# When weights are split while a layer norm's first half is turned: a hold with two levels

## The chip, the cores and the metric

The kernel runs on one core of a Trainium2 chip. The metric is the device time of one execution in microseconds (us). Before the change it is 2224.89 us, the median of 3 runs (2224.24 to 2225.13).

A core has engines that work through their own queues in order and wait for each other by semaphores: TensorE (PE, matrix products; PEld is its weight load), VectorE (DVE), ScalarE (ACT), GpSimd (POOL) and SyncE (SP), which here only issues DMAs.

## The reference, cut to what matters

One layer of an encoder over 256 rows of 2048 columns, in float32:

```python
x = layer_norm(ALPHA * x + 0.5 * swiglu(x, ffn1_w1, ffn1_w3, ffn1_w2), ln1_g, ln1_b)
mix = hybrid_mixer(x, w_in, b_gates, conv_w, norm_g, w_up_m, w_up_sb, w_out)
x = layer_norm(ALPHA * x + mix, ln2_g, ln2_b)
x = layer_norm(ALPHA * x + 0.5 * swiglu(x, ffn2_w1, ffn2_w3, ffn2_w2), ln3_g, ln3_b)
x = x + sigmoid(x @ w_ple_gate) * (p @ w_ple_proj)
```

`layer_norm` needs the mean and the variance of a whole row of 2048, so nothing that follows a norm can start for a row before the last column of that row is there. `swiglu` has an inner width of 5632.

## The kernel before, in words

**Products.** The 256 rows are two halves of 128 (t = 0, the first half, and t = 1, the second). A weight matrix is cut into tiles of 256 by up to 512 (512 KB), called weights below; each is used by one unit for each half. A float32 product is made of three products of a shorter format: every operand is split into a hi part (its rounded value) and a lo part (the rest), and a unit is two times three matmuls: hi by hi (L1115), hi by lo of the weight (L1116), lo of the activation by hi (L1117). Weights are split by `split_one`: ACT casts the raw tile to hi (L1064), DVE subtracts to get lo (L1068). Activations lie transposed in `actT` tiles, one for 512 columns (a chunk, c = 0 to 3) of one half; two weights use one chunk.

**Order.** The program is recorded by a Python scheduler that writes the units for PE in a fixed list and, between two units, whatever else is due by its planned clock (`Sched`, `DELAY`). Since every engine works in the order of recording, this decides what stands ahead of what on DVE and ACT. After each unit `splits_due` records splits as long as the number of split weights that still have a use (`splits`) is below a limit from `limits`: 5 in a feed-forward stage, 6 in the mixer, 11 within 8 weights of a border between stages, and 8 while `held[0]` is set. A unit whose weight isn't split yet forces it (`split_one` in the main loop). `loads` records the DMAs of raw weights up to another limit; it is called from `split_one`.

**A norm.** There are three: norm 1 between the first feed-forward part and the mixer, norm 2 between the mixer and the second feed-forward part, norm 3 between that and the last stage. Ahead of a norm, the last 8 units of the first half come before the last 8 of the second half for norms 1 and 3; after it, the first 8 weights are used for the first half, then for the second. For each half: DVE adds the finished product onto `xres` (L548, or L926 at norm 2) and takes statistics of 512 columns (L413); after the fourth, `finish` records BN_AGGR (L419), a square root on ACT (L238, out `rstd`), the reciprocal (L422) and the four scalings (L426). Then `turn` records for each chunk four transposes on PE (L436, into a PSUM bank `ms`), four ACTIVATEs on ACT (L238, scale and shift), the cast to hi on ACT (L442), and, 2.6 us later by the planned clock, the lo part on DVE (L444). `finish` sets `held[0]`, and the eighth lo part (`self.left == 0`) clears it. So splits of the next stage's weights are recorded between the steps of the norm, up to 8.

**The last stage** starts with four small products for each half (`w_ple_proj`, one weight each), whose results ACT copies from PSUM (L971); only then come the products of the normed rows with `w_ple_gate`.

Of the kernel before, what the change touches and what calls it, by code (L numbers as in the profile page):

```python
# [31 lines left out]
RAW_FFN, RAW_MIX, RAW_EDGE, RAW_HELD = 16, 5, 4, 8  # L32
SPLIT_FFN, SPLIT_MIX, SPLIT_EDGE, SPLIT_HELD = 5, 6, 11, 8
# [147 lines left out]
def kernel(  # L181
# [25 lines left out]
    def temp():  # L207
        sched.until(lambda: temps[0] < TEMP_BUFS)
        temps[0] += 1
        return temp_pool.tile([P, COL], F32, name="temp", tag="temp")  # L210

    def drop(n=1):
        temps[0] -= n

    def misc(shape):
        return ps_pool.tile(shape, F32, name="ms", tag="ps")
# [1 line left out]
    def big(shape=(P, 1024)):  # L218
        return page_pool.tile(list(shape), F32, name="big", tag="page")

    pages, held = [0], [False]

    def act_tile():
        pages[0] += 1
# [11 lines left out]
    def activate(out, in_, func, **kw):  # L236
        use_table(func)
        nc.scalar.activation(out, in_, func, **kw)  # L238
# [35 lines left out]
    def whole(act, c, t):  # L274
        if c not in act.whole:
            act.whole[c] = big()
            pages[0] += 1
        return act.whole[c][:, t * COL:(t + 1) * COL]

    def finished(act, c, t):  # L280
        act.mark(c, t, 4)
        if act.forms and all(act.ready(c, h) for h in range(TT)):
            sched.spawn(form_turn(act, c), DELAY["form"] + 3.0 * c)
# [97 lines left out]
    class Norm:  # L381
# [35 lines left out]
        def finish(self, t):  # L417
            mv = small.tile([P, 2], F32, name="mv", tag="mv")
            nc.vector.bn_aggr(out=mv[:], in_=self.stats[t][:])  # L419
            rstd = small.tile([P, 1], F32, name="rstd", tag="rstd")  # L420
            activate(rstd[:], mv[:, 1:2], ACT.Sqrt, bias=eps[:, 0:1])
            nc.vector.reciprocal(out=rstd[:], in_=rstd[:])  # L422
            held[0] = True
            for c in range(4):
                xs = xres[t][:, c * COL:(c + 1) * COL]
                nc.vector.tensor_scalar(out=xs, in0=xs, scalar1=mv[:, 0:1], scalar2=rstd[:, 0:1],  # L426
                                        op0=ALU.subtract, op1=ALU.mult)
                sched.spawn(self.turn(t, c), DELAY["ln_turn"] + DELAY["ln_step"] * c)
            return
            yield  # L430

        def turn(self, t, c):
            act = self.act
            ps = misc([P, 4, P])
            for k in range(4):
                nc.tensor.transpose(ps[:, k], xres[t][:, (4 * c + k) * P:(4 * c + k + 1) * P], ident[:])  # L436
            y = whole(act, c, t) if act.forms else temp()[:]
            for k in range(4):
                g, b = (self.gb[:, i, 4 * c + k:4 * c + k + 1] for i in range(2))
                activate(y[:, k * P:(k + 1) * P], ps[:, k], ACT.Identity, scale=g, bias=b)  # L440
            dst, y = act.get(c, t), y.rearrange("q (k s) -> q k s", s=P)
            nc.scalar.copy(dst[:, 0], y)  # L442
            yield DELAY["ln_low"]
            nc.vector.tensor_tensor(out=dst[:, 1], in0=y, in1=dst[:, 0], op=ALU.subtract)  # L444
            if not act.forms:
                drop()
            finished(act, c, t)
            self.left -= 1
            if self.left == 0:
                held[0] = False  # L450
                sched.spawn(self.rows(), self.delay)

        def rows(self):
# [21 lines left out]
    def ffn(w1, w3, w2, act, norm, skew=True, ahead=()):  # L475
# [9 lines left out]
        def up(c):  # L485
            s = {}

            def gate(ps, t):
                s[t] = temp()
                activate(s[t][:], ps, ACT.Silu)  # L490

            def hidden(ps, t):
                nc.vector.tensor_tensor(out=s[t][:], in0=ps, in1=s[t][:], op=ALU.mult)
                sched.spaced(turn(s[t], c, t), DELAY["h"] + 2.0 * t, TURN_GAP)

            return group(w1, range(0, D, 2 * P), c * COL, COL, act, gate), group(w3, range(0, D, 2 * P), c * COL, COL, act, hidden)

        def up7(c):
# [5 lines left out]
            def done(m, banks):  # L504
                ps = {k: v["ps"][:] for k, v in banks.items() if v}
                if m == 5:
                    e = temp()
                    nc.scalar.copy(e[:], ps["E"])
                    banks["B"]["ps"], banks["W"]["ps"] = seeded
                    both(banks["B"]["ps"][:], ps["X"], e[:], ALU.subtract)  # L510
                    drop()
                elif m == 6:
                    nc.scalar.copy(banks["W"]["ps"][:], ps["B"])
                elif m == 4:
                    s[1] = temp()
                    nc.scalar.copy(s[1][:], ps["E"])
                elif m == 2:
                    s[0] = temp()
                    sched.spawn(silu(s[0], ps["X"]), DELAY["silu"])
                elif m == 7:  # L520
                    both(s[1][:], ps["W"], s[1][:], ALU.add)
                    sched.spawn(silu(s[1], s[1][:]), DELAY["silu"])
                elif m == 3:
                    nc.vector.scalar_tensor_tensor(out=s[0][:], in0=ps["B"], scalar=-1.0, in1=s[0][:],
                                                   op0=ALU.mult, op1=ALU.mult)
                    sched.spaced(turn(s[0], c, 0), DELAY["h"], TURN_GAP)
                    sched.spawn(late(ps["W"]), DELAY["late"])
# [6 lines left out]
            def late(w):  # L534
                nc.vector.scalar_tensor_tensor(out=s[1][:], in0=w, scalar=-1.0, in1=s[1][:],
                                               op0=ALU.mult, op1=ALU.mult)
                sched.spaced(turn(s[1], c, 1), DELAY["h"], TURN_GAP)
                return
                yield
# [74 lines left out]
    def sb_columns(ps, t, first, count):  # L614

        for which in range(3):
            lo, hi = max(first, 8 * which), min(first + count, 8 * which + 8)
            if lo >= hi:
                continue
            name = ("sq", "sk", "sv")[which]  # L620
            src = ps[:, (lo - first) * DS:(hi - first) * DS]
            if which == 2:
                if (name, t) not in st:
                    st[name, t] = big()
                cs = slice((lo - 16) * DS, (hi - 16) * DS)
                nc.scalar.copy(st[name, t][:, cs], src)
                flags.update((name, t, h - 16) for h in range(lo, hi))
            else:
                stage = temp()
                nc.scalar.copy(stage[:, :(hi - lo) * DS], src)  # L630
                sched.spawn(sb_turn(name, t, stage, lo - 8 * which, hi - lo), DELAY["sbt"])
# [238 lines left out]
    for n in (4, 4, 4, 4, 4, 2):  # L870
        program.extend(flat(group(w_in, range(0, D, 2 * P), sq0 + first * DS, n * DS, x1T,
                                  lambda ps, t, f=first, n=n: sb_columns(ps, t, f, n))))
# [145 lines left out]
    def limits(j):  # L1018

        if held[0]:  # L1020
            return RAW_HELD, SPLIT_HELD
        if any(-EDGE <= j - e < EDGE for e, _ in edges):
            return RAW_EDGE, SPLIT_EDGE
        mixer = [m for e, m in edges if e <= j][-1:] == [True]
        return (RAW_MIX, SPLIT_MIX) if mixer else (RAW_FFN, SPLIT_FFN)
# [4 lines left out]
    def loads(most=len(raws)):  # L1030
        while (pos["load"] < most and pos["raw"] < (4 if pos["at"] < 6 else limits(pos["split"])[0])
               and (mixing() or pages[0] + pos["raw"] + 2 * max(limits(pos["split"])[1], len(splits)) < PAGES - SPARE)):
            j = pos["load"]
            r = raws[j]
            r.tile = page_pool.tile([P, 2, COL], F32, name="raw", tag="page")
            for ks in pieces(j):
                nc.sync.dma_start(out=r.tile[:, ks, :r.cols], in_=r.src[:, ks])
                if j == 0 and ks.start == 0:
                    load_x(0, 1)
            if r.plus is not None:  # L1040
                nc.gpsimd.dma_start(out=r.tile[:, :, :r.cols], in_=r.plus, accum_op=ALU.add)
            pos["load"] += 1
            pos["raw"] += 1
# [33 lines left out]
    def splits_due():  # L1077
        most = pos["at"] + 3 if pos["at"] < 8 else len(weights)
        while pos["split"] < most and len(splits) < limits(pos["split"])[1]:
            split_one()  # L1080
# [74 lines left out]
```

## Time and profile before

| | before |
|---|---|
| median of 3 runs | 2224.89 us |
| the profiled execution, its own time | 2225.94 us |
| its span, first to last instruction | 2224.2 us |
| PE busy | 2201.7 us (99%) |
| DVE busy | 1684.0 us (76%) |
| ACT busy | 1268.5 us (57%) |
| POOL busy | 187.2 us (8%) |
| chain that ended last: PE's share | 95% |
| mean granted TensorE clock | 0.996 |

The profiled execution is 1.05 us above the median, and 1.74 us of its time lie outside the span. PE is busy nearly throughout, so a change can take time away only where PE stands still or runs at a lower granted clock. Views by time show which lines stand there; a row of such a view has the start in us from the start of the span, the length, the engine, the line, the operation with its tiles and how many were merged, and in brackets the idle time before it and what ended it.

### The profile page before, as it was taken

Reading aid. Unit: us, or ns where it says so; the run is one execution under the profiler, and the core shown is the slowest. Engines: PE = TensorE matmul, PEld = TensorE weight load, DVE = VectorE, ACT = ScalarE, POOL = GpSimd, SP = SyncE. Lnnn points to the kernel's source line nnn. Section 1 sums busy time; section 2 is a strip of 40 time slices with the busy share of each in tenths; the row PEclk is TensorE's granted clock in tenths of the full one; section 3 lists DMA queues with packets and bytes.
Section 4 is the critical chain, followed back from the end, with each engine's and each line's share of the span. In section 5 each row is a group of like instructions: output and inputs, shape, how many; then the busy total and the mean of one; then the engine's idle time right before and its main releaser. Section 6 shows DMA issues by size and latency. Waiting matters only on the chain.

```text
span 2224.2 us, 27546 instructions
## 1 busy us (share of the span) xinstructions
PE 2201.7 (99%) x10068; PEld 1825.4 (82%) x10068; DVE 1684.0 (76%) x1859; ACT 1268.5 (57%) x1529; POOL 187.2 (8%) x167
## 2 busy tenths in 40 slices
PE   9999999999999999999999999999999999999999
PEld 7888888888887888888888888788888888888878
DVE  6889988888897784654545466499898989889774
ACT  6566665666565555535643354556665666566562
POOL 3111011100100000000000000011011101110000
PEclk9999999999999999999999999999999999999999
DMA  9899889987991765655566676579879998899532
GB/s 346 219 255 267 258 243 284 281 248 212 275 357 49 218 199 161 189 162 169 154 194 191 181 229 215 180 172 318 253 232 248 302 254 257 236 281 308 205 128 96
DMA packets 263049, 501.89 MB, mean 226 GB/s; under 512 B 15840, under 2 KB 24960, under 8 KB 262912
## 3 DMA queue, kind: packets, MB, share of 16 engines
q1 hardware_dynamic: 228096, 433.00, 58.9%
q0 software_dynamic: 34816, 67.12, 16.8%
q8 instruction: 79, 1.29, 0.2%
q14 instruction: 58, 0.48, 0.1%
HBM read 497.96 MB, written 2.10 MB: 225 GB/s over the span
## 4 chain that ended last, share of the span: by engine, by line
PE 95%; ACT 1%; DMA 1%; DVE 1%; issue 0%; DVEq 0%
PE mm L1117 27%; PE mm L1115 27%; PE mm L1116 27%; PE seeded L1115 4%; PE seeded L1117 4%; PE seeded L1116 4%; DMA raw<-in_ffn_w_dram 1%; PE ms L266 1%; DVE split L1068 1%; ACT temp L238 0%; ACT split L1064 0%; PE ms L436 0%; ACT big L238 0%; PE ms L823 0%; PE ms L846 0%
## 5 line engine op out<-in xcount | busy, mean ns | idle before, releaser
L1068 DVE TENSOR_TENSOR split<-raw,split 128x1024 fp32r<-128x1024 f32 (+1 forms) x1013 | 1183.5, 1204 | 317.5 <-ACT split L1064 300.8
L1064 ACT CAST split<-raw 128x1024 fp32r<-128x1024 f32 (+1 forms) x1013 | 1018.7, 1038 | 461.5 <-PE mm L1116 127.1
L1115 PE MATMUL mm<-split,actT 128*128 128x512 f32 (+2 forms) x2768 | 1078.3, 390 | 0.4 <-ACT split L1064 0.4
L1117 PE MATMUL mm<-split,actT 128*128 128x512 f32 (+2 forms) x2768 | 1067.6, 386 | 6.5 <-DVE actT L444 4.2
L1116 PE MATMUL mm<-split,actT 128*128 128x512 f32 (+2 forms) x2768 | 1066.5, 385 | 1.8 <-DVE split L1068 1.8
L1117 PEld LDWEIGHTS mm<-split,actT 128*128 128x128 f32 x2768 | 521.4, 188 | 113.2 <-DVE actT L444 5.4
L1116 PEld LDWEIGHTS mm<-split,actT 128*128 128x128 f32 x2768 | 522.0, 189 | 103.4 <-DVE split L1068 3.2
L1115 PEld LDWEIGHTS mm<-split,actT 128*128 128x128 f32 x2768 | 521.9, 189 | 101.4 <-issue 1.3
L336 POOL DMA_DIRECT2D raw<-in_ffn_w_dram x128 | 154.4, 1213 | 1308.9 <-DVE split L1068 747.3
L341 DVE TENSOR_TENSOR raw<-raw 128x1024 f32<-128x1024 f32 x128 | 155.9, 1218 | 10.7 <-DMA raw<-in_ffn_w_dram 10.7
L1115 PE MATMUL seeded<-split,actT 128*128 128x512 f32 x384 | 150.5, 392 | 0.0
L1117 PE MATMUL seeded<-split,actT 128*128 128x512 f32 x384 | 149.6, 389 | 0.0
L1116 PE MATMUL seeded<-split,actT 128*128 128x512 f32 x384 | 149.5, 389 | 0.0
L548 DVE SCALAR_TENSOR_TENSOR xres<-mm,xres 128x512 f32<-128x512 f32 x160 | 108.8, 685 | 16.3 <-PE mm L1117 16.3
L1117 PEld LDWEIGHTS seeded<-split,actT 128*128 128x128 f32 x384 | 72.1, 188 | 15.1
L1116 PEld LDWEIGHTS seeded<-split,actT 128*128 128x128 f32 x384 | 72.1, 188 | 14.7
L1115 PEld LDWEIGHTS seeded<-split,actT 128*128 128x128 f32 x384 | 72.1, 188 | 14.6
L268 ACT CAST actT<-ms 128x512 fp32r<-128x512 f32 x60 | 35.1, 587 | 69.0 <-PE ms L266 67.5
L271 DVE TENSOR_TENSOR actT<-ms,actT 128x512 fp32r<-128x512 f32 x60 | 41.0, 685 | 24.6 <-ACT actT L268 13.9
L238 ACT ACTIVATE temp<-mm 128x512 f32<-128x512 f32 (+1 forms) x38 | 21.8, 574 | 56.0 <-PE mm L1117 56.0
L238 ACT ACTIVATE big<-mm 128x512 f32<-128x512 f32 x20 | 12.0, 598 | 55.8 <-PE mm L1117 55.8
L234 ACT ACT_TABLE_LOAD x29 | 37.2, 1283 | 0.5
(137 smaller groups left out, 666.6 us busy)
## 6 DMA issues: line engine op xcount, KB each, us to landing
raw<-in_ffn_w_dram SPq DMA_DIRECT2D x527, 512.0 KB, 8.3
raw<-in_w_in_dram SPq DMA_DIRECT2D x168, 512.0 KB, 3.7
raw<-in_ffn_w_dram POOLq DMA_DIRECT2D x128, 512.0 KB, 9.6
raw<-in_w_out_dram SPq DMA_DIRECT2D x32, 512.0 KB, 4.9
raw<-in_w_ple_gate_dram SPq DMA_DIRECT2D x24, 512.0 KB, 5.8
raw<-in_w_up_m_dram SPq DMA_DIRECT2D x16, 512.0 KB, 4.2
raw<-in_w_up_sb_dram SPq DMA_DIRECT2D x16, 512.0 KB, 4.1
raw<-in_w_ple_gate_dram SPq DMA_DIRECT2D x16, 256.0 KB, 5.1
```

The source lines that it names most:

```text
L234: nc.scalar.preload_act_table_set(table[0])
L238: nc.scalar.activation(out, in_, func, **kw)
L268: nc.scalar.copy(dst[:, 0], ps[:])
L271: nc.vector.tensor_tensor(out=dst[:, 1], in0=ps[:], in1=dst[:, 0], op=ALU.subtract)
L336: nc.gpsimd.dma_start(out=raw.tile[:, :, :cols], in_=src.src, accum_op=ALU.add)
L341: nc.vector.tensor_tensor(out=a.tile[:, :, :cols], in0=a.tile[:, :, :cols], in1=b.tile[:, :, :cols], op=ALU.add)
L548: nc.vector.scalar_tensor_tensor(out=xs, in0=ps, scalar=0.5, in1=xs, op0=ALU.mult, op1=ALU.add)
L1064: nc.scalar.copy(hi[:, ks], r[:, ks])
L1068: nc.vector.tensor_tensor(out=lo[:, ks], in0=r[:, ks], in1=hi[:, ks], op=ALU.subtract)
L1115: nc.tensor.matmul(ps, hi, w[0][:, k, :u.cols], start=first, stop=False, skip_group_check=u.onto)
L1116: nc.tensor.matmul(ps, hi, w[1][:, k, :u.cols], start=False, stop=False, skip_group_check=u.onto)
L1117: nc.tensor.matmul(ps, lo, w[0][:, k, :u.cols], start=False, stop=last, skip_group_check=u.onto)
```

## The change

`held[0]` becomes a level: 0 (no norm under way), 1 (from the first half's statistics) or 2 (from the second half's statistics, or once four of the eight lo parts are done, whichever is recorded first). At level 1 the limit on splits is 0, at level 2 it is 8 as before. The limit on raw tiles stays 8. A unit whose weight isn't split still forces it.

```diff
-    pages, held = [0], [False]
+    pages, held = [0], [0]
...
             nc.vector.reciprocal(out=rstd[:], in_=rstd[:])
-            held[0] = True
+            held[0] = 1 + t
...
             self.left -= 1
+            if self.left == 4 and held[0] == 1:
+                held[0] = 2
             if self.left == 0:
-                held[0] = False
+                held[0] = 0
...
         if held[0]:
-            return RAW_HELD, SPLIT_HELD
+            return RAW_HELD, SPLIT_HELD if held[0] == 2 else 0
```

The two new lines in `turn` shift the numbers of all lines behind them by two (L548 becomes L550, L1068 L1070). PE, POOL and SP get the same instructions in the same order; on DVE and ACT the order changes at the three norms and nowhere else.

On DVE at norm 1, before, from the first half's scaling (`xres_86` is the first half, `xres_87` the second):

```order
L426 TENSOR_SCALAR xres_86<-xres_86,mv,rstd 128x512 x4
L548 SCALAR_TENSOR_TENSOR xres_87<-mm,xres_87 128x512
L413 BN_STATS stats<-xres_87 128x6
L548 SCALAR_TENSOR_TENSOR xres_87<-mm,xres_87 128x512
L413 BN_STATS stats<-xres_87 128x6
L1068 TENSOR_TENSOR split<-raw,split 128x1024 x2
L548 SCALAR_TENSOR_TENSOR xres_87<-mm,xres_87 128x512
L413 BN_STATS stats<-xres_87 128x6
L444 TENSOR_TENSOR actT<-temp,actT 128x512
L1068 TENSOR_TENSOR split<-raw,split 128x1024
L444 TENSOR_TENSOR actT<-temp,actT 128x512
L1068 TENSOR_TENSOR split<-raw,split 128x1024
```

And in the changed program, from behind the same scaling:

```order
L550 SCALAR_TENSOR_TENSOR xres_87<-mm,xres_87 128x512
L413 BN_STATS stats<-xres_87 128x6
L444 TENSOR_TENSOR actT<-temp,actT 128x512 x2
L550 SCALAR_TENSOR_TENSOR xres_87<-mm,xres_87 128x512
L413 BN_STATS stats<-xres_87 128x6
L444 TENSOR_TENSOR actT<-temp,actT 128x512
L419 BN_AGGR mv<-stats 128x2
L422 RECIPROCAL rstd<-rstd 128x1
L426 TENSOR_SCALAR xres_87<-xres_87,mv,rstd 128x512 x4
L1070 TENSOR_TENSOR split<-raw,split 128x1024 x5
L444 TENSOR_TENSOR actT<-temp,actT 128x512 x5
```

The four splits that stood between the lo parts, and the one behind the second half's scaling, now stand together behind that scaling. Norm 2 changes in the same way (two lo parts stand ahead of the second half's last addition, five splits behind its scaling). It is the second half's statistics that end level 1 at all three norms: the first half's fourth lo part comes behind the five splits.

On ACT at norm 3, before, from the second half's square root (`rstd`; L971 are the copies of the small products):

```order
L238 ACTIVATE rstd<-mv,eps 128x1
L1064 CAST split<-raw 128x1024
L971 COPY big<-mm 128x512 x2
L1064 CAST split<-raw 128x1024
L971 COPY big<-mm 128x512
L238 ACTIVATE temp<-ms,gb 128x128 x4
L442 CAST actT<-temp 128x512
L971 COPY big<-mm 128x512
```

And in the changed program:

```order
L238 ACTIVATE rstd<-mv,eps 128x1
L1066 CAST split<-raw 128x1024 x5
L973 COPY big<-mm 128x512 x2
L1066 CAST split<-raw 128x1024
L973 COPY big<-mm 128x512
L238 ACTIVATE temp<-ms,gb 128x128 x4
L442 CAST actT<-temp 128x512
L973 COPY big<-mm 128x512
L238 ACTIVATE temp<-ms,gb 128x128 x4
L442 CAST actT<-temp 128x512
L1066 CAST split<-raw 128x1024
L973 COPY big<-mm 128x512
```

Five casts instead of one now stand between the square root and the first copies; the other four stood between the first half's chunks, ahead of the root.

## The prediction

> **What bounds the kernel now.** PE is busy nearly all the time (table above), so I first asked whom PE waits for, longest first.
>
> ```profile
> PE ms L436 <- ACT split L1064: 5.3, 1, 5.3
> PE mm L1117 <- DVE actT L444: 4.2, 2, 2.7
> PE ms L436 <- DVE xres L426: 3.1, 1, 3.1
> ```
>
> The three longest waits (total us, times, longest) all belong to norms: the transposes L436 and the first use of a lo part, L444. Next I read PE by time at each norm. Norm 1, from the first matmul behind the border to the second half's first transposes:
>
> ```profile
> 703.20 0.39 PE L1115 MATMUL mm<-split,actT 128*128 128x512 f32 x1
> ...
> 706.56 0.79 PE L1117 MATMUL mm<-split,actT 128*128 128x512 f32 x1 [2.74 <-DVE actT L444]
> ...
> 713.19 0.60 PE L436 MATMUL ms<-ident,xres 128*128 128x128 f32 x4
> ```
>
> Norm 2, to the second group of transposes:
>
> ```profile
> 1413.31 0.39 PE L1115 MATMUL mm<-split,actT 128*128 128x512 f32 x1
> ...
> 1422.68 1.12 PE L436 MATMUL ms<-ident,xres 128*128 128x128 f32 x4 [3.14 <-DVE xres L426]
> ...
> 1426.15 0.60 PE L436 MATMUL ms<-ident,xres 128*128 128x128 f32 x4
> ```
>
> Norm 3, from the first small product to the third group of transposes:
>
> ```profile
> 2110.64 0.39 PE L1115 MATMUL mm<-split,actT 128*128 128x512 f32 x1
> ...
> 2114.49 0.39 PE L1117 MATMUL mm<-split,actT 128*128 128x512 f32 x1
> 2120.15 1.09 PE L436 MATMUL ms<-ident,xres 128*128 128x128 f32 x4 [5.27 <-ACT split L1064]
> ...
> 2126.49 0.60 PE L436 MATMUL ms<-ident,xres 128*128 128x128 f32 x4
> ```
>
> Undisturbed, a matmul starts every 3.85/17 = 0.2265 us (17 intervals from 2110.64 to 2114.49), so a unit of six takes 1.36 us; four transposes in between add 0.46 (after 1426.15 the next group came 1.82 us later). Now the time lost at each norm is what the stretch took less what its work needs. Norm 1: 9.99 us for three units (4.08), lost 5.91. Norm 2: 12.84 us for four units and one group of transposes (5.90), lost 6.94. Norm 3: 15.85 us for 30 matmuls and two groups (6.80 + 0.92 = 7.72), lost 8.13. **Together 20.98 us**: that is the most that the change can win.
>
> It is more than the waits named above, because the clock falls behind a stall. By stretches (us, then busy us and count of PE, PEld, DVE, ACT, POOL, then the granted clock, DMA share and GB/s):
>
> ```profile
> 30.10:33.50 3.40, 1.69 (x8) 1.09 (x7) 3.14 (x4) 1.94 (x2) 0.21 (x1) 1.00 1.05 387
> 702.50:705.90 3.40, 1.31 (x6) 0.75 (x4) 2.51 (x4) 3.37 (x7) 0.00 (x0) 1.00 0.00 0
> 705.90:712.70 6.80, 6.14 (x15) 4.79 (x16) 6.37 (x12) 2.56 (x4) 0.00 (x0) 0.50 0.00 0
> 1412.50:1415.90 3.40, 1.97 (x9) 1.33 (x8) 1.83 (x2) 3.37 (x7) 0.00 (x0) 1.00 0.81 265
> ```
>
> A stretch of 3.4 us with 1.31 us of busy PE is followed by half the clock for 6.8 us, which costs norm 1 the 3.0 us that 5.91 is above its stall of 2.90 (from 703.20 and two matmuls to 706.56). Stretches with 1.69 and 1.97 us busy were not followed by it. So a stall of up to 1.7 us in such a stretch keeps the clock, one of 2.1 doesn't.
>
> **Why PE waits.** DVE at norm 1:
>
> ```profile
> 700.35 1.23 DVE L1068 TENSOR_TENSOR split<-raw,split 128x1024 fp32r<-128x1024 f32 x1 [2.39 <-ACT split L1064]
> ...
> 705.83 0.68 DVE L444 TENSOR_TENSOR actT<-temp,actT 128x512 fp32r<-128x512 f32 x1
> ```
>
> DVE stands still for 2.39 us in front of a split whose cast waits its turn on ACT between two chunks' activations; the second half's additions and the lo parts are queued behind it and the next split. The first lo part is taken at 705.83, and PE goes on at 706.56, 0.05 us after its end. The change takes the splits from ahead of the lo parts and of the second half's statistics.
>
> **The change part by part.** No instruction is added or removed: 5 casts and 5 subtractions at each norm are moved. I work out when PE gets what it needs in the new order. The sequence that now follows the second half's last matmul stands in the trace already, at norm 3:
>
> ```profile
> 2116.72 0.68 DVE L548 SCALAR_TENSOR_TENSOR xres<-mm,xres 128x512 f32<-128x512 f32 x1
> ...
> 2119.46 1.92 DVE L426 TENSOR_SCALAR xres<-xres,mv,rstd 128x512 f32<-128x512 f32 x4
> 2121.29 1.22 DVE L1068 TENSOR_TENSOR split<-raw,split 128x1024 fp32r<-128x1024 f32 x1
> ```
>
> From the addition to the end of the scalings 4.57 us, and 1.22 for a split: 5.79, with some 0.04 at either end for the hand-over (0.05 at that lo part) 5.87 us.
>
> *Norm 1.* The second half's last matmul starts 0.23 ahead of 703.20 and takes 0.39: it ends at 703.36. The two lo parts first needed now stand behind the third addition, whose product ends two units and one group of transposes earlier (700.18); with 1.33 us for addition and statistics (0.72 + 0.61) the first lo part runs at 701.5 to 702.2, the second to 702.8. PE wants them at 703.65 and 706.4: **the stall of 2.9 goes, and with it the half clock**. What is late next is the fourth weight. Only three are split when the hold begins (before, four more came during it), and the fourth's lo part ends at 703.36 + 5.87 = 709.23. PE is there after three units, a group of transposes and one matmul: 703.20 + 4.08 + 0.46 + 0.23 = 707.97. **New wait 1.26 us.** The other four splits follow every 1.13 us or so, while PE takes 1.82 us for a unit with transposes, so they do not hold it. The first half's fourth lo part stands behind all five: about 709.2 + 4 x 1.14 + 0.7 = 714.4, and PE wants it at 714.9; that cover is thin, and without it the cost would be tenths.
>
> *Norm 2.* The same, with the last matmul ending at 1413.47 (0.23 ahead of 1413.31, and 0.39): split ready at 1419.34, PE there at 1413.31 + 4.77 = 1418.08, new wait 1.26 us, old loss of 6.94 gone.
>
> *Norm 3.* Here PE has four small products to do first, and stalls because the second half's scaling is late. Now: last matmul of the second half ends 2110.80, addition to first scaling 2.74 + 0.55, so the transposes can start at 2114.2, and PE wants them at 2114.7: stall gone. Next late is ACT:
>
> ```profile
> 2118.93 0.29 ACT L238 ACTIVATE rstd<-mv,eps 128x1 f32<-128x1 f32 x1 [4.22 <-DVE mv L419]
> 2119.13 1.03 ACT L1064 CAST split<-raw 128x1024 fp32r<-128x1024 f32 x1
> 2120.07 1.06 ACT L971 COPY big<-mm 128x512 f32<-128x512 f32 x2
> 2121.02 1.06 ACT L1064 CAST split<-raw 128x1024 fp32r<-128x1024 f32 x1
> 2121.97 0.59 ACT L971 COPY big<-mm 128x512 f32<-128x512 f32 x1
> 2122.44 1.53 ACT L238 ACTIVATE temp<-ms,gb 128x128 f32<-128x128 f32 x4
> 2124.00 0.62 ACT L442 CAST actT<-temp 128x512 fp32r<-128x512 f32 x1
> 2124.53 0.58 ACT L971 COPY big<-mm 128x512 f32<-128x512 f32 x1
> ```
>
> PE needs the copies to free PSUM banks. The root comes 2.21 us after the addition (2116.72 to 2118.93), so at 2113.05, the casts 0.2 later. A cast takes 0.95 of ACT, two copies 0.95, one 0.47, four activations with their cast 2.09. Five casts (4.75), two copies, a cast, a copy, a chunk, a copy, a chunk, a cast, and a copy of 0.58 until PE may start the first gate unit: 2113.25 + 4.75 + 0.95 + 0.95 + 0.47 + 2.09 + 0.47 + 2.09 + 0.95 + 0.58 = 2126.6. PE's own work up to there is 8 units and four groups (10.88 + 1.84) from 2110.64: 2123.4. **New waits 3.2 us in several pieces**, the first, about 1.6, in front of the fifth small product, behind the five casts.
>
> **The sum.** 20.98 - 1.26 - 1.26 - 3.2 = 15.3 us won. The profiled execution (2225.94) would take 2210.7; the median of the runs lies 1.05 below it, 2224.89 - 15.3 = **2209.6 us**. Unknown are the new waits, from nothing (2203.9) to as long as the stalls that they follow, with the clock (below). I take the worked-out values, whose durations are all of these places.
>
> **Does the clock hold?** The new waits of 1.26 are under the 1.7 that kept it. At norm 3 the first piece of 1.6 is close to that. [...]
>
> **Rivals.**
> *The clock falls at the new waits.* Half clock for 3.4 us costs up to 1.7. For it: the 1.6 at norm 3 with more pieces behind it. Against: 1.69 of 3.40 busy kept it. At norm 3 alone, one or two stretches: 2211.3 to 2213; at all three norms, one each: 2214.7.
> *Another wait behind the five casts.* The second half's activations start four casts (3.8 us) later on ACT. At norm 1 its first lo part, next on DVE behind the one of 714.4, would be ready near 715 and is wanted at 717.6 (709.23 + 1.13 + 3 x 1.82 + 1.36 + 0.45); were that cover gone, up to about 2 us at norms 1 and 2 each: 2211.6 to 2213.6.
> *Loads come late, and the second feed-forward part waits for them.* This one ends slower. In the built program the second of these loads at norm 2 waits for a page that a later matmul frees:
>
> ```profile
> 1389.63 0.88 SPq L1037 DMA_DIRECT2D raw<-in_ffn_w_dram  x2
> ```
>
> ```profile
> 1401.45 0.39 PE L1116 MATMUL mm<-split,actT 128*128 128x512 f32 x1
> ```
>
> It can start only at 1401.84, up to 12.2 us later, and SP's queue behind it too. If that stage were bound by its loads, norm 2's gain would go and 12.2 come: 2224.9 - 4.65 (norm 1) - 4.9 (norm 3) + 12.2 = 2227.6. It decides only if the cover is under 12.2 us: the load is now cast as the fifth, at about 1413.51 + 2.21 + 0.2 + 4 x 0.95 = 1419.7, 17.9 us after its new start.
> *The hold frees nothing* (the lo parts wait for something else): 2224.9. The order speaks against it.
>
> **How the numbers follow.** Forecast (2208 to 2211) 0.73, clock 0.14, casts 0.06, loads 0.04, nothing 0.03. The range: 2207.5, where about half of norm 3's and a bit of the other new waits vanish, to 2214.7, the clock at all norms; about 0.15 is left outside. A measurement here tells about 0.2% (4.45 us) from no change. Faster by that is everything under 2220.4: 0.92; the loads in part and the last case are the same, 0.05; slower 0.03.
>
> **What would show it.** PE's waits for L444 and L426 at norms 1 and 2 gone, one wait of about 1.3 us for a split's lo part in their place; at norm 3 waits for L973 (L971 before) of some 3 us in all; the granted clock whole at all three norms; PE's idle time in the second feed-forward part unchanged. Wrong would be: half clock after a new wait, new waits over 2 us at norms 1 and 2, or PE waiting for raw tiles behind norm 2.

## The result, and the profile after

The changed kernel takes **2211.05 us**, the median of 4 runs (2211.00 to 2211.37); the kernel before, in 4 runs of the same comparison, 2225.01 us (2224.24 to 2225.59). The ratio is 0.9938, 95% interval 0.9921 to 0.9955: 13.96 us less, where 15.3 were forecast.

| | before | after |
|---|---|---|
| median | 2225.01 us | 2211.05 us |
| the profiled execution, its own time | 2225.94 us | 2211.03 us |
| its span | 2224.2 us | 2209.3 us |
| PE busy | 2201.7 us | 2194.2 us |
| mean granted TensorE clock | 0.996 | 1.0 |

PE's waits in the changed kernel (total us, times, longest):

```profile
PE mm L1118 <- DVE split L1070: 4.3, 5, 1.1
PE mm L1117 <- ACT big L973: 2.4, 3, 1.5
```

The waits for L436 and L444 that headed this view are gone. In their place stand waits for a weight's lo part (two of the five are at norms 1 and 2, the others in the feed-forward parts, as before) and, at norm 3, waits for the copies out of PSUM. PE by time, norm 1, then norm 2, then norm 3:

```profile
702.82 0.39 PE L1117 MATMUL mm<-split,actT 128*128 128x512 f32 x1
...
706.90 0.60 PE L436 MATMUL ms<-ident,xres 128*128 128x128 f32 x4
707.26 0.48 PE L1117 MATMUL mm<-split,actT 128*128 128x512 f32 x1
708.87 0.50 PE L1118 MATMUL mm<-split,actT 128*128 128x512 f32 x1 [1.12 <-DVE split L1070]
709.20 0.40 PE L1119 MATMUL mm<-split,actT 128*128 128x512 f32 x1
```

```profile
1414.46 0.50 PE L1118 MATMUL mm<-split,actT 128*128 128x512 f32 x1 [1.12 <-DVE split L1070]
```

```profile
2108.52 0.50 PE L1117 MATMUL mm<-split,actT 128*128 128x512 f32 x1 [1.47 <-ACT big L973]
...
2112.99 0.50 PE L1117 MATMUL mm<-split,actT 128*128 128x512 f32 x1 [0.46 <-ACT big L973]
...
2116.48 0.50 PE L1117 MATMUL mm<-split,actT 128*128 128x512 f32 x1 [0.44 <-ACT big L973]
```

From the border's first matmul (702.82) to the transposes (706.90) are 4.08 us: exactly three units, so nothing of the old 5.91 is left there. Then comes one wait, at the fourth weight's lo part, as forecast. The clock stays whole in the stretches that hold these waits (us, then busy us and count of PE, PEld, DVE, ACT, POOL, then granted clock, DMA share, GB/s):

```profile
705.00:708.40 3.40, 2.74 (x15) 2.02 (x13) 3.00 (x8) 3.16 (x5) 0.00 (x0) 1.00 0.03 5
1411.60:1415.00 3.40, 2.28 (x12) 1.70 (x11) 3.40 (x6) 3.40 (x5) 0.00 (x0) 1.00 0.03 13
...
2107.90:2111.30 3.40, 2.78 (x14) 2.27 (x15) 3.40 (x4) 3.40 (x8) 0.00 (x0) 1.00 0.41 145
```

DVE at norm 1 shows the new order at work:

```profile
701.14 1.28 DVE L444 TENSOR_TENSOR actT<-temp,actT 128x512 fp32r<-128x512 f32 x2
...
705.57 0.17 DVE L422 RECIPROCAL rstd<-rstd 128x1 f32<-128x1 f32 x1 [0.36 <-ACT rstd L238]
705.77 1.92 DVE L426 TENSOR_SCALAR xres<-xres,mv,rstd 128x512 f32<-128x512 f32 x4
707.60 5.76 DVE L1070 TENSOR_TENSOR split<-raw,split 128x1024 fp32r<-128x1024 f32 x5
```

The first lo part runs at 701.14 instead of 705.83. Between the second half's last statistics and its scalings only one lo part is left, and no split. ACT at norm 3 shows where the new waits there come from, the five casts ahead of the copies:

```profile
2103.17 4.82 ACT L1066 CAST split<-raw 128x1024 fp32r<-128x1024 f32 x5
2107.89 1.06 ACT L973 COPY big<-mm 128x512 f32<-128x512 f32 x2
```

To compare kernels I take the time between the same two PE instructions around each norm: from the first matmul of the prediction's stretches (703.20, 1413.31 and 2110.64 in the trace of before) to a matmul behind the disturbance (716.60, 1432.08 and 2134.01). Each number is the difference of two start times:

| stretch of | norm 1 | norm 2 | norm 3 |
|---|---|---|---|
| before | 13.40 | 18.77 | 23.37 |
| after | 8.91 | 13.24 | 18.57 |
| won | 4.49 | 5.53 | 4.80 |
| forecast | 4.65 | 5.68 | 4.93 |

That is 14.82 of the 14.91 us between the two profiled executions.

### The profile page after: what moved, and what is told of

Same layout as the page of the kernel before. It is cut to its first block, busy times and chain, and to the rows that moved or that the text cites. A ratio compares the mean times of both kernels' runs of the same rounds, so it can differ in the third digit from the quotient of the medians.

```text
span 2209.3 us, 27558 instructions
## 1 busy us (share of the span) xinstructions
PE 2194.2 (99%) x10068; PEld 1820.1 (82%) x10068; DVE 1683.9 (76%) x1859; ACT 1268.7 (57%) x1529; POOL 187.5 (8%) x167
## 4 chain that ended last, share of the span: by engine, by line
PE 96%; DMA 1%; DVE 1%; ACT 1%; issue 0%; DVEq 0%; ACTq 0%
PE mm L1119 27%; PE mm L1117 27%; PE mm L1118 27%; PE seeded L1117 4%; PE seeded L1119 4%; PE seeded L1118 4%; DMA raw<-in_ffn_w_dram 1%; PE ms L266 1%; DVE split L1070 1%; PE ms L436 0%; ACT split L1066 0%; PE ms L825 0%; PE ms L848 0%; PE ms L776 0%; PE ms L788 0%
## 5 line engine op out<-in xcount | busy, mean ns | idle before, releaser
L1070 DVE TENSOR_TENSOR split<-raw,split 128x1024 fp32r<-128x1024 f32 (+1 forms) x1013 | 1182.3, 1203 | 298.8 <-ACT split L1066 284.5
L550 DVE SCALAR_TENSOR_TENSOR xres<-mm,xres 128x512 f32<-128x512 f32 x160 | 108.7, 684 | 22.0 <-PE mm L1119 22.0
```

The source lines that it names most:

```text
L550: nc.vector.scalar_tensor_tensor(out=xs, in0=ps, scalar=0.5, in1=xs, op0=ALU.mult, op1=ALU.add)
L1070: nc.vector.tensor_tensor(out=lo[:, ks], in0=r[:, ks], in1=hi[:, ks], op=ALU.subtract)
```

## The experiments

All diffs are against the changed kernel. `edges[k][0]` is the number of the first weight behind norm k+1.

**One norm at a time.** Three kernels; elsewhere the splits go on as before the change. The condition is that of `norm1_only`; `norm3_only` has `j < edges[2][0]`, `norm2_only` has `not edges[1][0] <= j < edges[2][0]`.

```diff
-            return RAW_HELD, SPLIT_HELD if held[0] == 2 else 0
+            return RAW_HELD, SPLIT_HELD if held[0] == 2 or j >= edges[1][0] else 0
```

> The new level holds the splits at norm 1 only; at norms 2 and 3 they stand as before the change. Between the kernel before (2225.0 us) and the changed one (2211.05 us) the stretch of norm 1 became 4.49 us shorter, that of norm 2 5.53, that of norm 3 4.80. Theory (each norm pays for itself): 2225.0 - 4.5 = 2220.5 us; PE's wait for L444 at norm 1 gone, one wait of 1.3 to 1.4 us for the fourth weight's lo part, norms 2 and 3 with their stalls and half clock of before. Rival (the second feed-forward part is bound by its loads, so that time won ahead of it is taken back there): PE's wait for a split near 1985 us, 0.4 us before, grows to as much as 4.9 us, and the time comes out at up to 2225. A small part of this is already seen: with 10.45 us won ahead of it that wait grew from 0.4 to 0.8.

> The new level holds the splits at norm 3 only. Theory (each norm pays for itself): 2225.0 - 4.8 = 2220.2 us, PE's waits at norm 3 for the copies L973 of 2.4 us in all, as in the changed kernel, and the 0.4 us wait for a split near 1990 us as before the change, since nothing was won ahead of it. Rival (the order alone decides, the clock is a lottery of the execution): the waits are the same, but a stretch at half clock of 3.4 us comes or goes at norms 1 and 2 against the kernel before, and the time differs from 2220.2 by 1.7 us or a multiple of it.

> The new level holds the splits at norm 2 only. Theory (each norm pays for itself; norms 1 and 3 alone won 4.7 and 4.45 us of the 14.3 between the medians of before, 2225.3, and after, 2211.05): 2225.3 - 5.1 = 2220.2 us, PE's wait for L426 at norm 2 gone and one of 1.4 us for the fourth weight in its place, norms 1 and 3 as before the change. Rival (part of the gain at one norm depends on another norm being changed too, by when loads or pages come free): the three single gains do not add up to 14.3, and this run is over 2221.2 or under 2219.2.

Measured: norm 1 alone 2220.62 us (2219.55 to 2221.37, 10 runs), norm 3 alone 2220.87 (2220.02 to 2221.68, 10 runs), both beside 2225.32 for before (19 runs, 2224.47 to 2227.09); norm 2 alone 2218.97 (2218.22 to 2220.13, 8 runs) beside 2225.23 (11 runs). In the profiles the changed norm's stretch is 8.91, 13.25 and 18.57 us, the same as in the changed kernel to 0.01: there each norm pays for itself. The medians add up less well: 4.70 + 6.26 + 4.45 = 15.4 us. `norm2_only` came out 0.2 us below 2219.2, the sign by which its rival was to be known; its profiled execution, the slowest of its 8, took 2220.13, close to the 2220.2 expected. The other runs lie as much as 1.9 us lower, and there is no trace of them. The equal stretches speak against the rival, but what made those runs shorter is open; the clock (next experiment) is a candidate.

The rival of a take-back in the second feed-forward part falls with `norm3_only`. Its PE waits between 1960 and 2000 us:

```profile
PE mm L1118 <- DVE split L1070: 0.8, 1, 0.8
```

Nothing was won ahead of it there, and the wait is 0.8 us all the same, as in the changed kernel; it was 0.4 in the trace of before and isn't set by the change.

**The kernel before, profiled once more.** No edit.

> The kernel before, profiled once more. [...] Rival (the clock follows the stalls alone, by their length): the same three stretches of half clock, 17.1 us in all.

Measured: 2225.14 us, span 2223.3. PE's waits at norm 1, and the clock by stretch there and at norm 2:

```profile
706.52 0.50 PE L1117 MATMUL mm<-split,actT 128*128 128x512 f32 x1 [2.75 <-DVE actT L444]
...
712.59 0.66 PE L436 MATMUL ms<-ident,xres 128*128 128x128 f32 x4 [2.15 <-DVE xres L426]
```

```profile
701.60:705.00 3.40, 2.17 (x10) 1.45 (x8) 1.68 (x2) 3.34 (x8) 0.00 (x0) 1.00 0.16 57
705.00:708.40 3.40, 1.88 (x8) 1.58 (x9) 3.37 (x6) 2.23 (x3) 0.00 (x0) 1.00 0.00 0
...
1418.40:1421.80 3.40, 0.64 (x3) 0.19 (x1) 2.97 (x7) 0.75 (x2) 0.00 (x0) 1.00 0.47 136
1421.80:1425.20 3.40, 3.03 (x9) 2.57 (x10) 3.40 (x6) 2.32 (x6) 0.00 (x0) 0.50 0.07 23
```

The stall of norm 1 is as long as in the first trace (2.9 us), but here the clock stays whole at it and behind it (1.00), where the first trace has 0.50 for 6.8 us. PE gains little by it: it runs ahead and then waits 2.15 us for the second half's scaling. The stretch of norm 1 is 12.93 us instead of 13.40, that of norm 2 18.60, that of norm 3 23.29. Of the three stretches of half clock of the first trace (6.8, 3.4 and 6.8 us behind norms 1, 2 and 3) the first is missing, and the rival falls: the same stall in the same kernel was followed by half clock in one execution and not in the other.

**Only the subtractions held back.** The casts on ACT stand as before the change; DVE's part and the freeing of the raw tile wait for level 2 (`freed` is what stood at the end of `split_one`).

```diff
+    def subtract():
+        while late: late.pop(0)()
+    late = []
...
-            return RAW_HELD, SPLIT_HELD if held[0] == 2 else 0
+            return RAW_HELD, SPLIT_HELD
...
-            nc.vector.tensor_tensor(out=lo[:, ks], in0=r[:, ks], in1=hi[:, ks], op=ALU.subtract)
+            late.append(lambda: nc.vector.tensor_tensor(out=lo, in0=r, in1=hi, op=ALU.subtract)) if held[0] == 1 else nc.vector.tensor_tensor(out=lo[:, ks], in0=r[:, ks], in1=hi[:, ks], op=ALU.subtract)
...
+        late.append(lambda: freed(w)) if held[0] == 1 else freed(w)
...
     def splits_due():
+        if held[0] != 1: subtract()
```

> The casts on ACT stand where they stood before the change; only the four subtractions on DVE (and the freeing of the raw tile behind them) are held back from the first half's statistics to the second half's. Theory (the lo parts were held up by DVE's place in line, and the casts on ACT cost something of their own): at norms 1 and 2 the stall for L444 is gone, PE waits about 1.4 us for the second half's scaling (its square root stands behind casts on ACT) and about 1.8 us for the fourth weight's lo part; at norm 3 1.4 us for the scaling and next to nothing for the copies, since the casts no longer stand together in front of them. Together 3.2 + 3.2 + 1.6 = 8.0 us against 6.0 in the changed kernel: 2213 us with the clock whole, up to 2216 if two stretches fall to half clock. Rival A (what stands ahead on ACT is what held up the norms): stalls as before, 2225. Rival B (only DVE's order matters): norms 1 and 2 as in the changed kernel, 1.3 us each, and norm 3 without its waits: 2208.

Measured: 2213.53 us (2212.03 to 2213.81, 4 runs; the profiled execution is the lowest). Its stretches are 10.48, 14.83 and 16.45 us: 1.57 and 1.59 more than the changed kernel at norms 1 and 2 (1.9 expected), 2.12 less at norm 3 (1.9 expected). DVE, then ACT, then PE, at norm 1 (in this kernel L1073 is the subtraction, L1069 the cast, L1121 to L1123 the matmuls):

```profile
707.24 0.16 DVE L422 RECIPROCAL rstd<-rstd 128x1 f32<-128x1 f32 x1 [1.94 <-ACT rstd L238]
```

```profile
705.02 1.99 ACT L1069 CAST split<-raw 128x1024 fp32r<-128x1024 f32 x2
706.92 0.29 ACT L238 ACTIVATE rstd<-mv,eps 128x1 f32<-128x1 f32 x1
```

```profile
708.04 0.66 PE L436 MATMUL ms<-ident,xres 128*128 128x128 f32 x4 [0.88 <-DVE xres L426]
...
710.54 0.50 PE L1122 MATMUL mm<-split,actT 128*128 128x512 f32 x1 [1.62 <-DVE split L1073]
```

The stall for L444 is gone with DVE's order alone, so rival A falls. But DVE waits 1.94 us for the square root instead of 0.36, because the root stands behind two casts on ACT: the late scaling is what the casts cost at norms 1 and 2, and rival B falls. At norm 3, where the change puts five casts together ahead of the copies, leaving them where they were is the better order by 2.1 us.

**Two splits ahead, then one.** At level 1 the next weights may be split after all, as far as the fifth (`two_ahead`) or the fourth (`one_ahead`, with `< 4`).

```diff
-            return RAW_HELD, SPLIT_HELD if held[0] == 2 else 0
+            return RAW_HELD, SPLIT_HELD if held[0] == 2 or any(0 <= j - e < 5 for e, _ in edges) else 0
```

> As the changed kernel, but two more weights (the fourth and the fifth of the next stage) may be split from the first half's statistics on; before the change it was four. Theory (the split whose subtraction stands on DVE ahead of the lo parts is what stalls PE, and a stall of over 2.1 us in a 3.4 us stretch halves the clock): the wait of 1.3 us for the fourth weight is gone, the stall for L444 is back, 3.2 us at norm 1 and 1.8 at norm 2, and 3.3 us for the scaling at norm 3, with 2.0 of copies behind it: 10.7 us of waits against 6.0, 2215.8 us, and half clock of 3.4 to 6.8 us behind norms 1 and 3 but not norm 2, 1.7 to 6 us more: 2217.5 to 2222. [...] Rival B (the fourth and fifth split fit into idle time of DVE, and the harm came from the last two only): waits gone at norms 1 and 2, 2208.5.

> As the changed kernel, but one more weight, the fourth of the next stage, may be split from the first half's statistics on (two brought the stall of 2.9 us at norm 1 back). Theory (DVE has room ahead of the lo parts for one split, 2.2 us of idle time before the second half's third addition, and none for a second): the waits of 1.4 us for the fourth weight at norms 1 and 2 go, some 0.3 us of bits stay at norm 1, norm 3 wins 0.2: 2211.05 - 1.1 - 1.4 - 0.2 = 2208.4 us, clock whole. Rival A (each split ahead delays the lo parts by as much as the next): at norm 1 a wait for L444 of about half of 2.9, 1.5 us, takes the place of the 1.4: 2209.7 to 2211. Rival B (what is won ahead of the second feed-forward part is taken back there by a wait for a load): 2211, with the wait for a split near 1979 us grown from 0.8 to 3.

Two ahead: 2215.67 us (2214.72 to 2218.73, 4 runs; the profiled one is the slowest). DVE, PE, and the clock at norm 1, and the clock at norm 2:

```profile
703.33 1.23 DVE L1070 TENSOR_TENSOR split<-raw,split 128x1024 fp32r<-128x1024 f32 x1 [1.79 <-ACT split L1066]
...
705.80 1.27 DVE L444 TENSOR_TENSOR actT<-temp,actT 128x512 fp32r<-128x512 f32 x2
```

```profile
706.52 0.79 PE L1119 MATMUL mm<-split,actT 128*128 128x512 f32 x1 [2.76 <-DVE actT L444]
```

```profile
1411.90:1415.30 3.40, 1.96 (x10) 1.30 (x8) 1.91 (x3) 3.37 (x7) 0.00 (x0) 1.00 0.80 261
...
702.30:705.70 3.40, 1.47 (x7) 0.89 (x5) 2.34 (x3) 3.01 (x7) 0.00 (x0) 1.00 0.00 1
705.70:709.10 3.40, 2.58 (x6) 2.10 (x7) 3.37 (x7) 0.00 (x0) 0.00 (x0) 0.51 0.00 0
```

The second split ahead brings the whole stall of norm 1 back, with half clock behind it (stretch 13.36, before 13.40); at norm 2 the stall is 1.6 us, without half clock (13.68); at norm 3 21.27. The profiled execution lies in the range expected, the median does not: its runs span 4 us, and the fastest has a mean granted clock of 1.0, the profiled one 0.997. The 2215.8 us that the waits alone give is the median to 0.1 us, but in the profiled execution the clock did fall, to 0.51, after a stretch that was 1.47 us busy.

One ahead: **2208.56 us** (2208.47 to 2208.62, 4 runs), 0.2 from the forecast, and 2.5 less than the changed kernel. The stretches are 7.71, 11.85 and 18.23 us. DVE at norm 1:

```profile
700.30 1.23 DVE L1070 TENSOR_TENSOR split<-raw,split 128x1024 fp32r<-128x1024 f32 x1 [2.40 <-ACT split L1066]
701.44 0.68 DVE L550 SCALAR_TENSOR_TENSOR xres<-mm,xres 128x512 f32<-128x512 f32 x1
...
702.77 1.28 DVE L444 TENSOR_TENSOR actT<-temp,actT 128x512 fp32r<-128x512 f32 x2
```

One split fits ahead of the lo parts: they start at 702.77, and PE wants the first about 703.6. PE has no wait at norms 1 and 2 in this trace. Rivals A and B fall.

**One ahead, and norm 3 relieved.** Norms 1 and 2 as in `one_ahead` (`edges[:-1]`); at norm 3 one split is recorded after each unit, and DVE makes the copies of the first three groups.

```diff
-            nc.scalar.copy(proj[g // 2, t][:, (g % 2) * COL:(g % 2 + 1) * COL], ps)
+            (nc.vector.tensor_copy if g < 3 else nc.scalar.copy)(proj[g // 2, t][:, (g % 2) * COL:(g % 2 + 1) * COL], ps)
...
-            return RAW_HELD, SPLIT_HELD if held[0] == 2 else 0
+            return RAW_HELD, SPLIT_HELD if held[0] == 2 or any(0 <= j - e < 4 for e, _ in edges[:-1]) else 0
...
-            split_one()
+            if split_one() or held[0] and pos['split'] > edges[-1][0]: break
```

> Three edits on the changed kernel: at norms 1 and 2 the fourth weight may be split from the first half's statistics on; at norm 3 splits are recorded one a unit instead of five together; and the copies of the small products out of PSUM are made by DVE for the first three groups of 512 columns, by ACT for the fourth. Theory (norm 3's waits are for copies that stand behind casts and activations on ACT): norms 1 and 2 win 1.1 and 1.4 us as with the first edit alone, and of norm 3's waits 2.6 of 3.4 us go, about 0.8 stays in front of one group of transposes: 2211.05 - 2.5 - 2.6 = 2206.0 us. Rival (DVE with its four scalings and the subtractions has no room for the copies either): the waits of norm 3 come back in front of L436 and behind L973 on DVE: 2208.5 us or more.

Measured: **2206.96 us** (2206.71 to 2207.35, 4 runs), the fastest of all; against before 0.9918, interval 0.9903 to 0.9932. PE's waits at norm 3:

```profile
PE ms L436 <- DVE big L973: 0.7, 1, 0.7
PE mm L1117 <- DVE big L973: 0.2, 1, 0.2
```

The waits for ACT are gone and 0.9 us for DVE are left, as expected, but the stretch is 16.57 us, 2.0 less than in the changed kernel and not 2.6. Its edits at norm 3 were not tried one by one, and it isn't shown which of them won the 2.0: `subtractions_only`, where ACT makes all the copies, has 16.45 there. In the profiled execution, the slowest of the four, norm 1 begins 0.35 us later than in that of `one_ahead` (703.48 against 703.13), behind work that was not touched.

## Why the prediction was right, and where its sum was off

**The loss at the norms.** That 20.98 us are lost there and that only this can be won stands: 14.82 of the 14.91 us between the profiles came from the three stretches, and the three single runs each won their own norm's part.

**The cause.** Right, and now tested: the lo parts waited for DVE's place in line. Holding back only DVE's subtractions removes the stall for L444, and letting two splits, casts and subtractions, back in restores it.

**The new waits.** Right in place and kind. The terms of 1.26 us were mis-sized: the stretches give 5.91 - 4.49 = 1.42 at norm 1 and 6.94 - 5.53 = 1.41 at norm 2. The wait itself was met (708.87, where 707.26 + 0.31 was the next start behind a group of transposes: 1.30); what the sum left out is that the matmul behind a wait starts 0.33 us later (708.87 to 709.20), not 0.23. The same 0.33 to 0.34 stands behind each wait of norm 3, where the 3.2 became 8.13 - 4.80 = 3.33. Together 0.44 us.

**From the profile to the median.** This step cost the most; the median of 2211.05 us lies just above the 2208 to 2211 that the prediction held likeliest, and within its range. The sum took the 1.05 us by which before's profiled execution lay above its median for an offset that would stay. Profile to profile the change won 14.91 us, 0.35 from the forecast; the other 0.95 of the miss of 1.3 is that before's profiled execution lay 0.93 us above the 2225.01 of the 4 runs beside the changed kernel's, and the changed kernel's own lies 0.02 below its median. Before's 4 runs scatter by 1.35 us (2.6 in 19 others), after's 4 by 0.4. About half of that excess is seen in the second profile of before: the stretch of norm 1 is 0.47 us shorter where the clock stays whole.

**What the half clock costs.** Here a reason was wrong, though the total was not. The prediction put the 3.0 us at norm 1 beyond its stall of 2.90 down to the half clock. Where the clock stays whole (`before_again`, and `norm3_only` with 12.92 us), the stretch is 0.47 us shorter, no more: PE then waits 2.15 us for the second half's scaling, which the slow clock had hidden. `norm2_only`, with the old order at norm 1 and 3.4 us at half clock behind it, has 12.93 as well. So two waits stood behind each other on DVE, and the change removed both. At norm 2 the half clock did cost: the same order took 17.21 us at full clock in `norm1_only`, 18.47 to 18.77 at half in three other traces, 1.3 to 1.6 us. At norm 3 both traces of the kernel before have 6.8 us of it, so its cost there stays open.

**Does the clock hold.** Right in the result (1.00 in all three stretches), incomplete in its limit of 1.7 us for a stall. At norm 2 of `norm1_only` PE waits 3.1 us for L426, as it did in the trace of before (3.14 us), and the clock stays whole, where before has 0.50 for 3.4 us behind the wait:

```profile
1412.70:1416.10 3.40, 2.20 (x9) 1.20 (x7) 3.37 (x6) 0.04 (x1) 0.00 (x0) 1.00 0.16 12
1416.10:1419.50 3.40, 1.47 (x9) 1.29 (x10) 3.00 (x9) 2.00 (x5) 0.00 (x0) 1.00 0.42 142
1419.50:1422.90 3.40, 3.40 (x21) 2.84 (x20) 2.19 (x3) 3.34 (x10) 0.00 (x0) 1.00 0.38 93
```

So the length of a stall alone doesn't tell whether the clock falls. In the two stretches that hold the wait here PE is idle for 1.20 and 1.93 us; in the trace of before all of it lies in one, 0.26 us busy of 3.40 (1419.30 to 1422.70). What decides between the two outcomes was not shown. The trace of before records half clock from 705.91, 1422.71 and 2119.03 us, for 6.83, 3.41 and 6.83 us.

**The rivals.** Clock: did not come (1.00 at all three norms). Second-half lo parts behind five casts: PE had no wait for them. Loads late: SP issued the loads of that place later, but nothing waited for them. SP in the changed kernel, where before had issued two at 1389.63:

```profile
1396.98 2.75 SPq L1039 DMA_DIRECT2D raw<-in_ffn_w_dram  x5
```

Between 1391 and 1401 us these five are all, and PE's only wait of that part is the 0.8 us near 1980 that `norm3_only` has too. That the hold frees nothing fell with the result.

## What to carry to other kernels

Work for the next stage that is recorded between the steps of a reduction should be counted against the idle time of the engine's queue at that place: here DVE had room for one split ahead of the lo parts, not for two, and the best version (2206.96 us) came from asking the same of each engine at each norm. Holding work back on two engines at once can pay on one and cost on the other, so try each engine's part alone. And before a profile's excess over the median is carried through a sum, ask whether the change removes the very thing that varies.

## What the runs showed that was not expected

The granted clock makes this kernel, with its stalls of 2.9 us and more at the norms, a lottery: the same stall halves the clock in one execution and not in another. Behind the wait of 2.7 to 2.8 us for L444 at norm 1 there were 6.8 us of half clock in the first trace of before, 3.4 us in `norm2_only`, and none in `before_again` and `norm3_only`. Nor does the busy time of a stretch of 3.40 us tell the cases apart: 1.47 us of it was followed by a clock of 0.51 in `two_ahead` (702.3 to 705.7) and by 1.00 in `norm1_only` (1416.1 to 1419.5). With no such stall left, the scatter of 4 runs shrank from 1.35 us (the kernel before) to 0.4 (the changed one) and 0.15 (`one_ahead`). And half the clock can cost next to nothing, 0.47 us for 6.8 us of it at norm 1, where PE would only have run into the next wait.
